# Attention scores: high parts above low parts, and the second product over 64 rows

## The chip, the cores and the metric

The kernel runs on one core of a Trainium2 chip. The metric is the device time of one execution in microseconds; the time before the change is 663.08 us, the median of two runs (663.04 and 663.12). Everything that the text says of single instructions comes from one further execution that the hardware profiler recorded.

## The reference

The reference is a one-layer encoder over 1024 positions (a grid of 16 rows by 64 columns) with 1024 channels: an embedding LayerNorm, one input projection, a neighbourhood attention with 8 heads of 64 channels, a bidirectional gated recurrence, two branch projections with sigmoid gates, an output projection, and a final LayerNorm. All of it is float32. The part that the change touches is the scores of the attention:

```python
q_rows = (q * scale).reshape(B, rows, GRID_W, H, Dh).transpose(1, 0, 2, 3, 4)
...
s = jnp.einsum('bqhd,bqnhd->bhqn', q_row, k_g).astype(jnp.float32) + bias[None]
p = jax.nn.softmax(s, axis=-1).astype(v.dtype)
return jnp.einsum('bhqn,bqnhd->bqhd', p, v_g)
```

Every query of a head has a dot product over 64 channels with the keys of its window (8 rows by 16 columns of the grid); a bias is added, and the softmax over the window weights the values.

## The kernel before, in words

**Tiles.** The 1024 positions are cut into eight tiles of 128 (16 grid rows by 8 grid columns each). The window of a query lies in its own tile and the two beside it (`near`), so a tile's scores are a block of 128 queries by 384 keys, or by 256 keys in the first and the last tile; the bias holds a huge negative number outside the window.

**Two parts of a number.** [...] Most products of the kernel take three (`mm3`, line 129: high by high, low by high, high by low). The scores need two matmuls, because a head has only 64 channels and the array has 128 rows: the 128 rows hold both parts of q.

**Before the attention.** q and k of all heads are projected, split and stored to DRAM (`q_d`, `k_d`: per pair of heads 128 channels, then the part z, then the position).

**Loading a head.** `load_q` (line 925) brings q of one head as 128 rows of 1024 positions. The DRAM view is "(p z) s": row 2p is the high part of channel p, and row 2p+1 its low part. The same function loads the head's bias. `load_k` (line 933) brings k as 128 rows of two times 1024 positions. Rows 2p and 2p+1 hold the same data: the high part of channel p and behind it the low part; the copy is made by a broadcast view of one DMA. q and the bias have one buffer for even heads and one for odd heads; k has two buffers.

**The scores.** `score` (line 1102) issues two matmuls per head and tile into one PSUM bank. Both have the same 128 x 128 block of q as weights. The first has k's high part as the moving operand, so it sums (q high + q low) x k high; the second has k's low part and adds (q high + q low) x k low. That is four products of parts in two matmuls.

**The attention stage.** One loop over units (line 1236 on) writes down the order by hand, on every engine: nothing is reordered by a planner. A unit is one tile of one head: it holds the score of the next head, its bias and row minimum on VectorE (`biased`, line 1109, one DVE instruction out of PSUM), the exponential on ScalarE (`exped`), the transposes of the present head's probabilities on PE (`turned`), their split into two parts (`turned_hi` on ScalarE, `turned_lo` on VectorE), and their product with the values (`values`). Between these, PE does matmuls of the recurrence branch's projection (`filler`, tensor `mb`, line 133), 12 to 20 of them a head. The sums of the softmax are transposed once a head (`sums_turned`, line 1172), with 8 columns of weights.

**Queues.** Nearly all DMAs are issued by SyncE (SP), in program order, each issue waiting in that order for its buffer. At the first unit of head h SP issues the loads of head h+2 (`load_head`): q, bias, k, then the gate `za` of the pair in odd heads; the filler's loads (`wb`, `g`) follow. The scores of head h+2 begin eight units later, at the first unit of head h+1. The loads of heads 0 and 1 are issued in the stage before, at the slots around `HEAD_AT`.

Of the kernel before, what the change touches and what calls it, by code (L numbers as in the profile page):

```python
# [10 lines left out]
F32 = mybir.dt.float32  # L11
# [4 lines left out]
P = 128  # L16
S = 1024
# [3 lines left out]
DH = 64  # L21
# [26 lines left out]
HALVES = ((slice(0, 64), slice(64, P)), (slice(64, P), slice(0, 64)))  # L48
# [3 lines left out]
def near(t):  # L52

    return range(max(t - 1, 0), min(t + 2, NT))
# [13 lines left out]
def encoder_kernel(ctx, tc, x, gb1, gb, w_qk, w_v, w_s, w_ba, w_bb, w_gate, smalls, bias, w_out, out):  # L68
    nc = tc.nc
    V, A, G, PE, SP = nc.vector, nc.scalar, nc.gpsimd, nc.tensor, nc.sync  # L70
# [26 lines left out]
    q_d = dram.tile([H // 2, P, 2, S], F32, name="q_d")  # L97
    k_d = dram.tile([H // 2, P, 2, S], F32, name="k_d")
# [822 lines left out]
    def head_start():  # L921
        late["hd0"] = pool("hd0", "right")
        load_q(0)

    def load_q(h):
        hd = late["hd" if h % 2 else "hd0"]
        q = hd.tile([P, S], F32R, tag="qs", name=f"qs{h}")
        bt = hd.tile([P, BIAS_W], F32, tag="bias", name=f"bias{h}")
        SP.dma_start(q[:].bitcast(F32), q_d[h // 2][HALVES[h % 2][0]].rearrange("p z s -> (p z) s"))
        SP.dma_start(bt[:], bias[h])  # L930
        heads[h] = q, bt

    def load_k(h):
        k = late["hd"].tile([P, 2, S], F32R, tag="ks", bufs=2, name=f"ks{h}")
        SP.dma_start(k[:].rearrange("p z s -> p (z s)").bitcast(F32),
                     k_d[h // 2][HALVES[h % 2][0]].rearrange("p z s -> p (z s)").unsqueeze(1).to_broadcast([DH, 2, 2 * S]))
        heads[h] = heads[h][0], k, heads[h][1]

    def load_head(h):
        if h < H:  # L940
            load_q(h)
            load_k(h)
# [21 lines left out]
    for t, slot in enumerate(LATE_AT[1:]):  # L964
        at(slot, 1, lambda t=t: yb_load(t))
        at(slot + 2, 1, lambda t=t: yb_hi(t))
        at(slot + 3, 0, lambda t=t: yb_lo(t))
    at(HEAD_AT, 1, head_pool)
    at(HEAD_AT, 1, lambda: load_k(0))
    at(HEAD_AT, 1, lambda: load_head(1))  # L970
    at(HEAD_AT - 3, 1, head_start)
# [81 lines left out]
    for slot in range(7 * N_PAIR + 4):  # L1053
        p, k = divmod(slot, 7)
# [47 lines left out]
    def score(h, t):  # L1102
        q, k, _ = heads[h]
        keys = slice(near(t).start * P, near(t).stop * P)
        o = scs[h, t] = pst.tile([P, HALF], F32, tag="s", bufs=2, name=f"s{h}_{t}")
        for z in range(2):
            PE.matmul(o[:, :P * len(near(t))], q[:, t * P:(t + 1) * P], k[:, z, keys], start=z == 0, stop=z == 1)  # L1107

    def biased(h, t):

# [125 lines left out]
    for unit in range(-NT, H * NT + PV_LAG):  # L1236
        h, c = divmod(unit, NT)
# [32 lines left out]
        if -1 <= h < H - 1:  # L1270
            score(h + 1, SCORES[c])
# [44 lines left out]
    def ring(slot, name):  # L1316
        tag = RING[slot % 8]
        return pst.tile([P, HALF], F32, tag=tag, bufs=1 if tag[0] == "a" else 2, name=name)
# [300 lines left out]
    for slot in range(16 + len(plan)):  # L1619
# [17 lines left out]
        if slot < 16:  # L1637
# [3 lines left out]
            o = got[slot] = ring(slot, f"mb{j}{n}")  # L1641
# [6 lines left out]
        a, b, p = plan[slot - 16]  # L1648
# [4 lines left out]
        if slot < 16 + len(plan) - 1:  # L1653
            o = banksX[p] if a in ("a11", "s2", "s3", "a22") else banksW[p]
# [5 lines left out]
    p, x, w = 3, banksX[3], banksW[3]  # L1660
# [11 lines left out]
    for n, part in pieces[2:] + pieces[:2]:  # L1672
        z = zs[p, 1, n]
# [89 lines left out]
```

## Time and profile before

| | |
|---|---|
| median of the runs shown | 663.08 us |
| the profiled execution's own time | 663.5 us |
| its span, first to last instruction | 661.7 us |
| PE busy, share of the span | 649.5 us, 98% |
| weight loads (PEld), which overlap PE | 543.5 us, 82% |
| VectorE (DVE) | 521.6 us, 79% |
| ScalarE (ACT) | 389.0 us, 59% |
| GpSimd (POOL) | 396.7 us, 60% |
| mean granted TensorE clock | 0.996 |
| scores, line 1107: 128 matmuls | 31.7 us busy, mean 329 ns |
| scores' first weight load, last matmul start | 428.2 us, 521.7 us |

How to read it: a line gives the source line, the engine, the operation, the tensors (out<-in), the shapes and the count. For a weight load, `128*128` is rows by columns of the array that it fills. PE's matmuls are pipelined and their ends are modelled, so the step from one start to the next is a better measure of the cost of a matmul than its duration. A wait names the instruction whose end released it.

### The profile page before, as it was taken

How to read it: one execution, taken by the hardware profiler on the slowest of the kernel's cores; microseconds unless marked ns; L12 is line 12 of the kernel's file. 1: busy time of each engine (PE TensorE's matmuls, PEld its weight loads, DVE VectorE, ACT ScalarE, POOL GpSimd, SP SyncE). 2: the span in 40 equal slices, each digit the busy share in tenths (PEclk: the TensorE clock that was granted, in tenths of full speed). 3: DMA queues.
4: the chain of work that ended last, by engine and by line, in shares of the span. 5: the costliest groups of instructions: out<-in, count | busy, mean ns of one | idle time of the engine just before them, and what ended most of it. 6: DMA issues, size and time to landing. Idle time of an engine off the chain costs nothing.

```text
span 661.7 us, 9464 instructions
## 1 busy us (share of the span) xinstructions
PE 649.5 (98%) x3119; PEld 543.5 (82%) x3119; DVE 521.6 (79%) x860; ACT 389.0 (59%) x686; POOL 396.7 (60%) x311
## 2 busy tenths in 40 slices
PE   8999999999999999999999999999999999999994
PEld 7888888888888887888788888888898888888883
DVE  7978867786899599879987696277877876994776
ACT  5564433356786677777666834277777744573242
POOL 6799263434676476658556455013552549989857
PEclk9999999999999999999999999999999999999998
DMA  8747607033334133532361548898977298333023
GB/s 324 271 140 250 195 33 257 15 111 128 125 113 135 57 112 99 188 111 81 132 220 59 192 163 281 306 342 272 362 264 240 68 306 294 113 113 127 24 104 128
DMA packets 52482, 113.42 MB, mean 171 GB/s; under 512 B 5505, under 2 KB 9937, under 8 KB 50897
## 3 DMA queue, kind: packets, MB, share of 16 engines
q1 hardware_dynamic: 51968, 112.28, 49.0%
q8 instruction: 25, 0.41, 0.2%
q10 hardware_dynamic: 464, 0.53, 0.2%
q14 instruction: 25, 0.20, 0.1%
HBM read 77.11 MB, written 35.68 MB: 170 GB/s over the span
## 4 chain that ended last, share of the span: by engine, by line
PE 86%; DVE 7%; POOL 2%; issue 1%; ACT 1%; DMA 1%; POOLq 0%; DVEq 0%; ACTq 0%
PE a L133 32%; PE s L133 12%; PE mb L133 12%; PE x L133 6%; PE w L133 5%; PE v L327 4%; PE s L1107 3%; PE acc L1155 3%; PE pt L1129 3%; PE q L133 2%; PE g L805 2%; POOL x L260 1%; DVE ws_l L127 1%; DVE uc L763 1%; PE tp L271 1%
## 5 line engine op out<-in xcount | busy, mean ns | idle before, releaser
L133 PE MATMUL a<-ht_h,ws_h 128*128 128x512 f32 x136 | 53.1, 391 | 0.0
L133 PE MATMUL a<-ht_l,ws_h 128*128 128x512 f32 x136 | 52.9, 389 | 0.0
L133 PE MATMUL a<-ht_h,ws_l 128*128 128x512 f32 x136 | 52.9, 389 | 0.0
L133 PE MATMUL a<-b_l,wa_h 128*128 128x512 f32 x136 | 52.9, 389 | 0.0
L133 PE MATMUL a<-b_h,wa_h 128*128 128x512 f32 x136 | 52.9, 389 | 0.0
L133 PE MATMUL a<-b_h,wa_l 128*128 128x512 f32 x136 | 52.9, 389 | 0.0
L1117 DVE CUSTOM_DVE_ANT_0 sc<-s,bias 128x384 f32<-128x384 f32 (+1 forms) x64 | 33.5, 523 | 20.3 <-PE s L1107 11.4
L1136 ACT CAST pt_h<-pt 128x384 fp32r<-128x384 f32 x64 | 29.0, 453 | 23.8 <-PE pt L1129 19.3
L1122 ACT ACTIVATE p<-sc,summ 128x384 f32<-128x384 f32 (+1 forms) x64 | 37.9, 592 | 5.4 <-DVE summ L1117 5.0
L133 PE MATMUL mb<-ya,wb_h 128*128 128x512 f32 x128 | 39.7, 390 | 0.1
L913 POOL CAST wb_h<-wb 128x512 fp32r<-128x512 f32 x9 | 7.0, 781 | 47.2 <-DMA wb<-in_w_bb_dram 47.2
L127 DVE TENSOR_TENSOR pt_l<-pt,pt_h 128x384 fp32r<-128x384 f32 x64 | 33.3, 520 | 1.9 <-ACT pt_h L1136 1.6
L127 POOL TENSOR_TENSOR ht_l<-t,ht_h 128x512 fp32r<-128x512 f32 x16 | 21.9, 1406 | 18.2 <-ACT ht_h L313 18.2
L1521 POOL TENSOR_TENSOR z<-z,gb 128x512 f32<-128x512 f32 (+2 forms) x23 | 27.7, 1218 | 8.5 <-ACT z L1516 7.5
L327 PE MATMUL v<-wv,b_h 128*128 128x512 f32 x128 | 32.4, 395 | 0.4 <-ACT b_h L426 0.4
L1107 PE MATMUL s<-ks,qs 128*128 128x384 f32 (+1 forms) x128 | 31.7, 329 | 0.0
L133 PEld LDWEIGHTS a<-ht_h,ws_h 128*128 128x128 f32 x136 | 25.5, 188 | 5.9 <-issue 0.5
L1129 PEld LDWEIGHTS pt<-ident,p 128*128 128x128 f32 x176 | 23.1, 140 | 8.3
L133 PEld LDWEIGHTS a<-ht_l,ws_h 128*128 128x128 f32 x136 | 25.5, 188 | 5.3
L133 PEld LDWEIGHTS a<-b_h,wa_l 128*128 128x128 f32 x136 | 25.5, 188 | 5.3
L133 PEld LDWEIGHTS a<-b_h,wa_h 128*128 128x128 f32 x136 | 25.5, 188 | 5.3
L133 PEld LDWEIGHTS a<-b_l,wa_h 128*128 128x128 f32 x136 | 25.5, 188 | 5.3
(542 smaller groups left out, 2258.9 us busy)
## 6 DMA issues: line engine op xcount, KB each, us to landing
ks<-k_d SPq DMA_DIRECT2D x8, 1024.0 KB, 7.6
h_d<-x SPq DMA_DIRECT2D x8, 512.0 KB, 2.9
v_d<-vs SPq DMA_DIRECT2D x8, 512.0 KB, 3.2
q_d<-q SPq DMA_DIRECT2D x8, 512.0 KB, 3.2
ga_d<-ga SPq DMA_DIRECT2D x16, 256.0 KB, 2.1
gb_d<-gb SPq DMA_DIRECT2D x16, 256.0 KB, 2.4
k_d<-k SPq DMA_DIRECT2D x8, 512.0 KB, 5.1
qs<-q_d SPq DMA_DIRECT2D x8, 512.0 KB, 5.2
```

What stands on the lines that cost most here:

```text
L127: eng.tensor_tensor(lo, full, hi.bitcast(F32), ALU.subtract)
L133: PE.matmul(o, a, b, start=first and i == 0, stop=last and i == len(prods) - 1, skip_group_check=not (first and last))
L327: PE.matmul(vos[i][:], a, wv[kind == "w"][k][:], start=vn[i] == 0, stop=vn[i] == 23)
L805: PE.matmul(o[:, n, :], w[:, 2 * d + b, :], us[b][:, n * HALF:(n + 1) * HALF], start=z == 0, stop=z == 1)
L913: G.tensor_copy(hi[:], st[:])
L1107: PE.matmul(o[:, :P * len(near(t))], q[:, t * P:(t + 1) * P], k[:, z, keys], start=z == 0, stop=z == 1)
L1117: V.tensor_tensor_reduce(s[:, :w], o[:, :w], heads[h][2][:, b0:b0 + w], -1.0, 3.0e38, ALU.add, ALU.min, accum_out=sums[h][0][:, t:t + 1])
L1122: A.activation(probs[h % 2][t][:], scs.pop((h, t))[:, :w], AF.Exp, bias=sums[h][0][:, t:t + 1], scale=-1.0, accum_out=sums[h][1][:, t:t + 1])
L1129: PE.transpose(tp[:, n * P:(n + 1) * P], probs[h % 2][t][:, z * P:(z + 1) * P], ident[:])
L1136: A.copy(pt[0][:, span(b)], tps[h, b][:, :P * len(near(b))])
L1155: PE.matmul(acc[n][:, lo - n * HALF:hi - n * HALF], vvs[h // 2][:, b, h % 2, :], pt[:, a:a + hi - lo], start=b in (1, 6) and z == 0, stop= ...
L1521: G.tensor_tensor(z, z, gbs[c, n][:, part], (ALU.mult, ALU.add)[c])
```

## The change

Three places change. `load_q` fills rows 0 to 63 with the high part of q and rows 64 to 127 with the low part, by two DMAs. `load_k` fills rows 0 to 63 and rows 64 to 127 with the same 64 channels of k (high part, then low part), again by two DMAs in place of one with a broadcast view. `score` takes its first matmul over all 128 rows, as before, which sums (q high + q low) x k high; the second is taken over rows 0 to 63 alone, which adds q high x k low. The product q low x k low is no longer in the sum. Numbers and sizes of the matmuls' columns, all buffers, and the order of the work on each engine stay as they are.

```diff
@@ -926,14 +926,15 @@
         hd = late["hd" if h % 2 else "hd0"]
         q = hd.tile([P, S], F32R, tag="qs", name=f"qs{h}")
         bt = hd.tile([P, BIAS_W], F32, tag="bias", name=f"bias{h}")
-        SP.dma_start(q[:].bitcast(F32), q_d[h // 2][HALVES[h % 2][0]].rearrange("p z s -> (p z) s"))
+        for z, rows in enumerate((slice(0, DH), slice(DH, P))):
+            SP.dma_start(q[rows].bitcast(F32), q_d[h // 2][HALVES[h % 2][0], z])
         SP.dma_start(bt[:], bias[h])
         heads[h] = q, bt
 
     def load_k(h):
         k = late["hd"].tile([P, 2, S], F32R, tag="ks", bufs=2, name=f"ks{h}")
-        SP.dma_start(k[:].rearrange("p z s -> p (z s)").bitcast(F32),
-                     k_d[h // 2][HALVES[h % 2][0]].rearrange("p z s -> p (z s)").unsqueeze(1).to_broadcast([DH, 2, 2 * S]))
+        for rows in (slice(0, DH), slice(DH, P)):
+            SP.dma_start(k[rows].bitcast(F32), k_d[h // 2][HALVES[h % 2][0]])
         heads[h] = heads[h][0], k, heads[h][1]
 
     def load_head(h):
@@ -1103,8 +1104,8 @@
         q, k, _ = heads[h]
         keys = slice(near(t).start * P, near(t).stop * P)
         o = scs[h, t] = pst.tile([P, HALF], F32, tag="s", bufs=2, name=f"s{h}_{t}")
-        for z in range(2):
-            PE.matmul(o[:, :P * len(near(t))], q[:, t * P:(t + 1) * P], k[:, z, keys], start=z == 0, stop=z == 1)
+        for z, rows in enumerate((slice(0, P), slice(0, DH))):
+            PE.matmul(o[:, :P * len(near(t))], q[rows, t * P:(t + 1) * P], k[rows, z, keys], start=z == 0, stop=z == 1)
```

## The prediction

> **What bounds the kernel now.** I read the page first: busy times, then the chain of work that ended last.
>
> ```profile
> span 661.7 us, 9464 instructions
> PE 649.5 (98%) x3119; PEld 543.5 (82%) x3119; DVE 521.6 (79%) x860; ACT 389.0 (59%) x686; POOL 396.7 (60%) x311
> PE 86%; DVE 7%; POOL 2%; issue 1%; ACT 1%; DMA 1%; POOLq 0%; DVEq 0%; ACTq 0%
> PE a L133 32%; PE s L133 12%; PE mb L133 12%; PE x L133 6%; PE w L133 5%; PE v L327 4%; PE s L1107 3%; PE acc L1155 3%; PE pt L1129 3%; PE q L133 2%; PE g L805 2%; POOL x L260 1%; DVE ws_l L127 1%; DVE uc L763 1%; PE tp L271 1%
> ```
>
> PE is busy for 98% of the span and holds 86% of the chain. The scores (L1107) are on the chain themselves, with 3%. A share over the whole span says little about one stage, so the next views are the stretches of the attention stage, 425 to 535 us, and the rows of the score matmuls.
>
> ```profile
> 445.00:455.00 10.00, 10.00 (x64) 9.02 (x63) 7.70 (x23) 7.83 (x23) 1.91 (x2) 1.00 1.00 336
> ...
> sum 110.00, PE 109.85 PEld 96.98 DVE 83.58 ACT 77.82 POOL 42.95; mean PE 9.99 PEld 8.82 DVE 7.60 ACT 7.07 POOL 3.90
> ```
>
> The columns are the stretch and its length, then busy time (and count) of PE, weight loads, DVE, ACT and POOL, then granted clock, DMA share and GB/s. PE works 109.85 of 110 us, at the full clock; the next engine, DVE, works 83.58. So in this stage a microsecond more or less on PE is a microsecond of the kernel, and what DVE, ACT or a transfer gains is worth nothing. The clock is already whole: a cooler array has nothing to win.
>
> ```profile
> L1107 PEld LDWEIGHTS s<-ks,qs x128: 186/188/193, 428.2 to 521.5; 128*128 128x128 f32 x128
> L1107 PE MATMUL s<-ks,qs x128: 277/338/423, 428.4 to 521.7; 128*128 128x384 f32 x96, 128*128 128x256 f32 x32
> L1107 PEldq EVENT_SEMAPHORE  x8: 51/51/51, 424.3 to 508.7; - x8
> ```
>
> There are 128 score matmuls, two for each of 64 scores. The change touches the second of each pair: 48 of 384 columns and 16 of 256.
>
> **Part 1: the second product over 64 rows.** The cost of a matmul in a full stream is the step from start to start.
>
> ```profile
> 472.29 0.40 PE L1107 MATMUL s<-ks,qs 128*128 128x256 f32 x2
> 472.53 0.40 PE L133 MATMUL mb<-yb_h,wb_l 128*128 128x512 f32 x1
> ...
> 475.18 0.52 PE L1107 MATMUL s<-ks,qs 128*128 128x384 f32 x2
> 475.53 0.39 PE L133 MATMUL mb<-yb_h,wb_h 128*128 128x512 f32 x1
> ```
>
> Two matmuls of 384 columns take 475.53 - 475.18 = 0.35 us, 0.175 each; two of 256 take 0.24, 0.12 each. The step follows the columns, and the columns stay. The weight load changes from 128x128 to 64x128. It lies beside the running matmul (the steps of 0.12 and 0.175 contain it), so a shorter one gains nothing. Bounds for a matmul of half the rows: at best it takes half of its step, 48 x 0.0875 + 16 x 0.06 = 5.2 us less in all; at worst it can't be overlapped with its full-row neighbours, which is the first rival below. The trace has no matmul of 64 rows, but two instructions with a part of the array. The nearer one in place, inside this stage, is the transpose of the softmax sums, whose weights fill 8 of 128 columns; the other, at the start of the program, fills 16 of 128 rows.
>
> ```profile
> 449.28 0.49 PE L1129 MATMUL pt<-ident,p 128*128 128x128 f32 x3
> 449.53 0.36 PE L1155 MATMUL acc<-pt_h,vv 128*128 128x256 f32 x1
> ...
> 450.66 0.49 PE L1129 MATMUL pt<-ident,p 128*128 128x128 f32 x3
> 450.99 0.27 PE L1174 MATMUL pt<-ident,sums 128*8 128x128 f32 x1
> 451.02 0.42 PE L1155 MATMUL acc<-pt_h,vv 128*128 128x384 f32 x1
> ```
>
> Without the odd transpose, three transposes and the next matmul's start are 0.25 us apart; with it, 0.36. So it costs 0.11, and that is what each ordinary transpose costs (450.99 - 450.66 is three steps of 0.11). Entering and leaving the 8-column shape adds nothing that can be read.
>
> ```profile
> 450.88 0.09 PEld L1174 LDWEIGHTS pt<-ident,sums 128*8 128x8 f32 x1
> 450.99 0.19 PEld L1155 LDWEIGHTS acc<-pt_h,vv 128*128 128x128 f32 x1
> ```
>
> The full weight load behind it starts at 450.99, together with the odd matmul, which is modelled to run for 0.27: it doesn't wait for that matmul's end.
>
> ```profile
> 2.84 0.31 PE L203 MATMUL clock<-zero 128*128 128x128 bf16 x1
> 3.08 0.18 PEld L414 LDWEIGHTS clock<-ident,gb_row 16*128 16x128 f32 x1 [0.20 <-issue]
> 3.11 0.26 PE L414 MATMUL clock<-ident,gb_row 16*128 16x16 f32 x1
> 3.29 0.10 PEld L203 LDWEIGHTS <-zero 128*128 128x128 bf16 x1
> ```
>
> Here rows are cut. The load of 16 rows starts at 3.08, before the full-row matmul ahead of it ends (2.84 + 0.31 = 3.15), and the next full-row load starts at 3.29, before the 16-row matmul ends (3.11 + 0.26 = 3.37). Neither direction shows a wait for an empty array, though the ends are modelled, the clock was still low there, and this is one instance. I take zero for the 64 second products, by the row inside the stage, and keep -5.2 us as the lower end.
>
> **Part 2: the loads.** For each head SP issues two DMAs more: one of q and one of k. The bytes stay: q 512 KB and k 1024 KB are written to the same rows in halves.
>
> ```profile
> L929 SPq DMA_DIRECT2D qs<-q_d x8: 315/320/587, 405.7 to 496.5; - x8
> L935 SPq DMA_DIRECT2D ks<-k_d x8: 527/535/693, 415.0 to 497.6; - x8
> ```
>
> The added issues take 0.32 + 0.54 = 0.86 us of SP for a head by the medians, if a half costs what the whole does. Behind them SP has the bias, k, the gate `za` and the filler's loads. Whether that costs time depends on how long SP idles afterwards.
>
> ```profile
> 416.68 0.59 SPq L935 DMA_DIRECT2D ks<-k_d  x1
> 419.26 0.32 SPq L706 DMA_DIRECT2D gb_d<-gb  x1
> ...
> 434.42 0.32 SPq L929 DMA_DIRECT2D qs<-q_d  x1
> 435.77 0.69 SPq L935 DMA_DIRECT2D ks<-k_d  x1
> 439.40 0.35 SPq L1179 DMA_DIRECT2D rs_d<-rs  x1
> ...
> 498.79 0.59 SPq L904 DMA_DIRECT2D wb<-in_w_bb_dram  x1
> 501.18 0.32 SPq L1017 DMA_DIRECT2D g<-gb_d  x1
> ```
>
> After k of head 2 SP is free from 436.46 to 439.40, 2.9 us. After the longest train of issues it is free from 499.38 to 501.18, 1.8 us. After the loads of heads 0 and 1 it is free from 417.27 to 419.26, 2.0 us, against three added issues there (k of head 0, q and k of head 1: up to 0.59 + 0.59 + 0.59 = 1.8 us). Each covers what is added; `za`, `wb` and `g` are issued up to 0.9 us later, and PE has no wait of any length for them in the stage now (its idle time is 0.15 of 110 us). The value on PE is zero. Without that cover it would be 0.86 x 8 = 6.9 us.
>
> Next, do q and k still land in time? They are issued a head ahead.
>
> ```profile
> DMA to landing us min/median/max: 4.9/7.6/9.1
> ...
> 446.80 0.19 PEld L1107 LDWEIGHTS s<-ks,qs 128*128 128x128 f32 x1
> ...
> 446.87 0.54 SPq L935 DMA_DIRECT2D ks<-k_d  x1
> ...
> 459.33 0.36 PEld L1107 LDWEIGHTS s<-ks,qs 128*128 128x128 f32 x2
> ```
>
> The first line is k's own landing time, the second the first weight load of head 2's scores; the last two are the issue and the first use of head 3's k. Head 2's k, issued at 435.77, has landed by 444.87 even with the longest landing, 1.9 us ahead of use. The second issues of q and k push the last half back by 0.32 + 0.69 = 1.0 us, so 0.9 us is left. Head 2 has 11.0 us from the issue of k to its use, head 3 has 12.5. So no wait appears, as long as a half with 64 rows moves at the pace of the whole. If not, it is the second rival.
>
> The first product of a head now has to see four transfers landed in place of two. One wait is already an instruction of its own, 51 ns long, once a head. Two more a head would be 16 x 0.051 = 0.8 us; the one before the first score ran at 424.3, 3.9 us ahead of it, and so beside older matmuls. I take zero, and 0.8 us as its upper end.
>
> **The sum.** 0 (columns) + 0 (part of the array) + 0 (SP) + 0 (waits) on the profiled execution's own 663.5 us, which is its span of 661.7 and 1.8 around it. The runs' median, 663.08, is 0.4 below this execution, so the forecast is 663.2 us, with 662 to 665 for this case alone: the 0.8 us of waits and as much again of SP's issues, above, and a microsecond below for what the rows don't resolve.
>
> **The rivals.**
>
> *First: changing between 128 and 64 rows stops the pipeline (slower).* If a weight load of another row count can't be made under the running matmul, it stands in the open, once on the way in and once on the way out: 128 times. By the transposes' step, which is as long as a weight load of 128 columns can be apart from the next, that is 0.11 us each, 14 us in all: 677 us. If the array must also run empty, a score matmul lasts 0.338 and its successor starts after 0.175, so 0.16 more, and the whole load of 0.188 behind it: 0.35 x 128 = 45 us, 708 us. It decides as soon as a switch costs more than 0.10 us. The two partial instructions above speak against it; for it speaks only that none of them has 64 rows amid a stream of 384 columns. [...] I give it 0.12 in full, and 0.05 to a part of it, such as one direction only (665 to 672 us).
>
> *Second: DMAs of 64 rows are slower, and the scores wait for k.* In the loads' stretch the engines move 336 GB/s at a share of 1.00. q and k, 1.57 MB by their shapes, take 4.7 us at that rate; at half of it 4.7 us more. Head 2 would then be late by 4.7 - 0.9 = 3.8 us at worst. With k's median landing of 7.6 us instead of 9.1 the lateness is 2.3 us, and 1.5 us less for a later head, 0.8 us. Over the six heads loaded within the stage that is 5 to 23 us: 668 to 686 us. The trace has a load of 64 rows, the softmax sums, beside loads of 128 rows and the same 256 KB, the gates `g`, in the same stage:
>
> ```profile
> DMA to landing us min/median/max: 3.4/5.9/6.2
> ...
> DMA to landing us min/median/max: 3.5/5.9/9.1
> ```
>
> The first is the 64-row load (rsb), the second the 128-row one (g). They land alike, so I give this 0.06. [...]
>
> *Third: half of the rows takes less time (faster).* Then up to 5.2 us go: 658 us, within 2%. Against it: the steps follow columns alone, and the partial transpose is no cheaper than a whole one. 0.05.
>
> **How the numbers follow.** Zero change 0.72; first rival 0.12 in full and 0.05 in part; second 0.06; third 0.05. The range 661 to 672 us holds the first case, the partial switch and the near ends of the second and third, about 0.8. This kernel's runs tell a change of 2% (13.3 us, beyond 676.3 or below 649.8) from none. Slower than that are the first rival in full and half of the second: 0.15. Nothing reaches 2% faster, 0.01. Within 2%: 0.84.
>
> **What would show it.** Right: the second score matmul listed with 64*128 and 64x384, steps of 0.175 into and out of it, PE still some 109.8 of 110 us busy in the stage, scores from 428 to 522 us. Wrong by the first rival: the 64-row weight load or the full one behind it starts only after the matmul before it, steps above 0.28 us around L1107, and PE or its weight loads idle by "issue". Wrong by the second: waits of PE or its weight loads on `ks<-k_d` at the start of a head, and landings above 11 us. Wrong by the third: a step near 0.09 us.

## The result and the profile after

The changed kernel takes 699.11 us (two runs, 697.86 and 700.36) against 663.08 before: 1.054 times as long, 95% interval 1.046 to 1.062. The forecast of 663.2 us, no change, was wrong by 36 us.

The page of the changed kernel, the lines that answer to those shown of before:

```profile
span 698.6 us, 9488 instructions
PE 682.9 (98%) x3119; PEld 549.2 (79%) x3119; DVE 521.8 (75%) x860; ACT 388.9 (56%) x686; POOL 396.6 (57%) x311
PE a L133 27%; PE mb L133 14%; PE s L133 10%; PE x L133 6%; PE s L1108 5%; PE w L133 5%; PE v L327 4%; PE acc L1156 3%; PE pt L1130 3%; PE q L133 2%; DVE ws_l L127 2%; DMA g<-gb_d 2%; PE g L805 2%; POOL x L260 1%; DVE uc L763 1%
```

PE has as many instructions as before and is still "98% busy": the added time is booked as work. Only the chain betrays a change, with the scores (now L1108) at 5% and a transfer that was not on it, `g<-gb_d`, at 2%.

The score matmuls of before, of after, and of the run with the row change alone (below), from the view of the tile `s`; the two times are the starts of the first and the last of them:

```profile
L1107 PE MATMUL s<-ks,qs x128: 277/338/423, 428.4 to 521.7; 128*128 128x384 f32 x96, 128*128 128x256 f32 x32
```

```profile
L1108 PE MATMUL s<-ks,qs x128: 278/391/687, 432.4 to 558.7; 128*128 128x384 f32 x48, 64*128 64x384 f32 x48, 128*128 128x256 f32 x16, 64*128 64x256 f32 x16
```

```profile
L1107 PE MATMUL s<-ks,qs x128: 277/381/443, 428.5 to 545.4; 128*128 128x384 f32 x48, 64*128 64x384 f32 x48, 128*128 128x256 f32 x16, 64*128 64x256 f32 x16
```

All of the loss lies here. The first score starts 432.4 - 428.4 = 4.0 us later. From first to last score it takes 126.3 us in place of 93.3, 33.0 more. After the last score both kernels have the same 140 us to go (661.7 - 521.7 and 698.6 - 558.7). Together they are the 36.9 by which the span grew, within the rounding of the views. The row change alone takes 116.9 us from first to last score, so of the 33.0 it explains 23.6, and 9.4 are left. These 9.4 lie in the first two heads: from the third head on, both runs take 15.65 us a head.

Two of these three parts are seen in the waits of the changed kernel from 425 to 565 us, and the third in the stretches:

```profile
PEld s L1108 <- issue: 15.7, 64, 0.5
DVE m L1031 <- DMA g<-gb_d: 11.3, 2, 10.7
PEld mb L133 <- issue: 10.6, 51, 0.3
...
PE s L1108 <- DVE m L1031: 4.0, 1, 4.0
```

```profile
435.00:445.00 10.00, 10.00 (x20) 5.42 (x20) 2.70 (x10) 3.43 (x10) 1.20 (x1) 0.50 0.47 169
445.00:455.00 10.00, 10.00 (x27) 6.33 (x26) 3.65 (x12) 2.76 (x9) 0.00 (x0) 0.52 0.59 160
...
465.00:475.00 10.00, 10.00 (x50) 7.05 (x50) 6.62 (x19) 6.21 (x19) 0.17 (x1) 1.00 0.85 209
```

First, each of the 64 scores' 64-row weight loads, and the full-row load behind most of them, starts after idle time that nothing else explains ("issue"). Second, once, PE waits 4.0 us for the instruction `m` of DVE, which frees a bank, and DVE waits for the gate g. Third, in the twenty microseconds after that the granted clock is 0.50 and 0.52 of full speed. "PE 10.00 of 10.00" is printed for all three stretches, with 20, 27 and 50 matmuls in them; the count and the clock tell what the busy time hides.

### The profile page after: what moved, and what is told of

Same layout as the page of the kernel before. It is cut to its first block, busy times and chain, and to the rows that moved or that the text cites. A ratio compares the mean times of both kernels' runs of the same rounds, so it can differ in the third digit from the quotient of the medians.

```text
span 698.6 us, 9488 instructions
## 1 busy us (share of the span) xinstructions
PE 682.9 (98%) x3119; PEld 549.2 (79%) x3119; DVE 521.8 (75%) x860; ACT 388.9 (56%) x686; POOL 396.6 (57%) x311
## 4 chain that ended last, share of the span: by engine, by line
PE 83%; DVE 9%; DMA 2%; POOL 2%; issue 2%; ACT 1%; POOLq 0%; DVEq 0%; ACTq 0%
PE a L133 27%; PE mb L133 14%; PE s L133 10%; PE x L133 6%; PE s L1108 5%; PE w L133 5%; PE v L327 4%; PE acc L1156 3%; PE pt L1130 3%; PE q L133 2%; DVE ws_l L127 2%; DMA g<-gb_d 2%; PE g L805 2%; POOL x L260 1%; DVE uc L763 1%
## 5 line engine op out<-in xcount | busy, mean ns | idle before, releaser
L1108 PE MATMUL s<-ks,qs 128*128 128x384 f32 (+3 forms) x128 | 48.4, 413 | 4.0 <-DVE m L1031 4.0
L1108 PEld LDWEIGHTS s<-ks,qs 128*128 128x128 f32 (+1 forms) x128 | 26.2, 205 | 20.8 <-issue 15.7
L1194 POOL TENSOR_TENSOR za<-za,rsb 128x512 f32<-128x512 f32 x8 | 10.2, 1290 | 41.5 <-DMA rsb<-rs_d 41.5
L1130 PE MATMUL pt<-ident,p 128*128 128x128 f32 x176 | 30.3, 276 | 0.0
```

The costliest lines, as they stand in the source:

```text
L1108: PE.matmul(o[:, :P * len(near(t))], q[rows, t * P:(t + 1) * P], k[rows, z, keys], start=z == 0, stop=z == 1)
L1130: PE.transpose(tp[:, n * P:(n + 1) * P], probs[h % 2][t][:, z * P:(z + 1) * P], ident[:])
L1194: G.tensor_tensor(gates[hp][:, halves[n]], gates[hp][:, halves[n]], rsb[hp][:, halves[n]], ALU.mult)
```

## The experiments

My theory (A) after seeing this: three separate causes. The change between 128 and 64 rows costs PE time at every score; transfers of 64 rows are slow and delay g; and the stall that follows lets the clock fall. The rivals: the row change does it all (B), the loads do it all (C), a 64-row matmul is itself slower (D).

**The row change alone, and the loads alone.** The first run keeps the loads of before and changes the second product; the second run keeps the loads of after and makes both products full.

```diff
-        for z in range(2):
-            PE.matmul(o[:, ...], q[:, t * P:(t + 1) * P], k[:, z, keys], ...)
+        for z, rows in enumerate((slice(0, P), slice(0, DH))):
+            PE.matmul(o[:, ...], q[rows, t * P:(t + 1) * P], k[rows, z, keys], ...)
```

> The loads of before, and the second score product over rows 0 to 63 alone (in this layout these are the high and the low part of channels 0 to 31; channels 32 to 63 are left out of that product). Theory A: after's 36 us are two things, the change between 128 and 64 rows (0.39 us for each of 64 scores by after's steps, 25 us) and, by itself, a stall of PE at 428 us with a low clock behind it, which comes from the loads by halves. Then this run takes 688 us (685 to 691), without the stall and at a clock of 1.00. Rival B: all of it comes from the change of rows, the low clock too: 699 us. Rival C: all of it comes from the loads: 663 us.

> The loads of after (q and k by halves of 64 rows), both score products over all 128 rows; nothing of the computation is left out. Theory A: PE idles about 4 us at 428 us while the gate g of the filler lands behind the halves of k, the clock falls to half and comes back sooner than in after, since full-row matmuls follow without gaps: 668 to 676 us. Rival B: 663 us. Rival C: 699 us.

The row change alone: 686.96 us, ratio 1.036 (1.034 to 1.038), at a clock of 0.995. That is 23.9 us, as theory A had it. The loads alone: 692.33 us (685.6 to 693.9), ratio 1.041 (1.035 to 1.047). The theory had 668 to 676, so the loads cost far more by themselves than I thought. PE's waits in that run, 440 to 560 us, say where:

```profile
PE s L1108 <- DMA ks<-k_d: 15.3, 5, 6.3
PE s L1108 <- issue: 3.0, 1, 3.0
```

The scores of five heads wait for k, up to 6.3 us; a sixth wait, of 3.0 us, stands at the same place of a head without a named cause. The two losses, 24 and 29 us, don't add up to the 36 of the changed kernel, which has no such wait. Its steps are longer, so a head lasts longer (15.65 us against 12.5 to 12.8 from first score to first score), and it starts its scores later; so k lands within it, and the one loss covers a part of the other.

**What of the row change costs.** Two runs with the loads of before: both products over 64 rows, and the second product over 96.

```diff
+        for z, rows in enumerate((slice(0, DH), slice(0, DH))):   # both over 64
+        for z, rows in enumerate((slice(0, P), slice(0, 96))):    # second over 96
```

> The loads of before, both score products over rows 0 to 63 (channels 32 to 63 are left out of the scores). It has twice the 64-row matmuls of the run with the second product alone, and as many changes of rows. Theory A, the change is what costs: as that run, 688 us, with a step of 0.175 us between the two 64-row matmuls. Rival D, a 64-row matmul costs more by itself: twice the loss, 713 us.

> The loads of before, the second score product over rows 0 to 95 (channels 48 to 63 are left out of that product). Theory A, in the form that the array's division costs: 96 rows don't fit into a half of the array, so the array stays whole and the run takes 663 us. Rival D, any matmul of fewer rows than its neighbours costs: 688 us.

Both over 64 rows: 686.21 us, ratio 1.035 (1.033 to 1.037). Twice the 64-row matmuls, the same loss: it goes with the changes, not with the matmuls. Over 96 rows: 663.07 us, ratio 1.000 (0.999 to 1.001), and the scores take as long as before:

```profile
L1107 PE MATMUL s<-ks,qs x128: 277/337/422, 428.3 to 521.8; 128*128 128x384 f32 x48, 96*128 96x384 f32 x48, 128*128 128x256 f32 x16, 96*128 96x256 f32 x16
```

So a matmul of fewer rows than its neighbours is not what costs, and rival D falls. That the array is divided for 64 rows was my theory's assumption: no view shows it, and no run between 64 and 96 rows shows where the cost sets in.

The price in place, PE and then its weight loads in the changed kernel around one score:

```profile
470.35 0.34 PE L1108 MATMUL s<-ks,qs 128*128 128x384 f32 x1
470.62 0.44 PE L1108 MATMUL s<-ks,qs 64*128 64x384 f32 x1
470.99 0.50 PE L133 MATMUL mb<-yb_l,wb_h 128*128 128x512 f32 x1
471.33 0.39 PE L133 MATMUL mb<-yb_h,wb_h 128*128 128x512 f32 x1
```

```profile
470.62 0.18 PEld L1108 LDWEIGHTS s<-ks,qs 64*128 64x128 f32 x1 [0.20 <-issue]
470.99 0.19 PEld L133 LDWEIGHTS mb<-yb_l,wb_h 128*128 128x128 f32 x1 [0.19 <-issue]
471.10 0.19 PEld L133 LDWEIGHTS mb<-yb_h,wb_h 128*128 128x128 f32 x1
```

The steps are 0.27, 0.37 and 0.34 us where before has 0.175, 0.175 and 0.23: 0.40 more for one way in and out, and 0.37 on average (23.6 / 64). Each weight load of the other kind starts together with its own matmul, 0.27 or 0.37 after the matmul ahead of it; in a stream of one kind it starts with the matmul ahead (the load of this score's first matmul at 470.23, as the matmul ahead of that one). So it is no longer made under the running matmul: the two overlap by 0.07 us (470.35 + 0.34 against 470.62), by the modelled end. What it waits for is not shown.

**What of the loads costs.** Three runs. The first has the layout and products of before with as many DMAs as after, each over 128 rows. The second is the loads alone, with the halves for rows 64 to 127 issued from ScalarE's queue. The third is the loads alone with the first two gates g issued ahead of head 1's loads, and no longer behind them.

```diff
+        for c in halves:                       # q in two DMAs of 128 rows
+            SP.dma_start(q[:, c]..., ...[:, c])
+        for z in range(2):                     # k in two DMAs of 128 rows
+            SP.dma_start(k[:, z, :]..., k_d[...][HALVES[...][0], z].unsqueeze(1).to_broadcast([DH, 2, S]))
...
+            (A if z else SP).dma_start(q[rows]..., ...)              # two queues
+            (A if rows.start else SP).dma_start(k[rows]..., ...)
...
+    for n in range(2):                         # early gates
+        at(HEAD_AT, 1, lambda n=n: g_load(1, 0, n))
     at(HEAD_AT, 1, lambda: load_head(1))
```

> The layout and the products of before, but q and k of a head each by two DMAs of all 128 rows (q by halves of its positions, k its high part and its low part), so as many issues and transfers as in after. Theory A: what makes after's loads slow is that a transfer of 64 adjacent rows moves at about 215 GB/s instead of 350 to 400. Then this run takes 663 us (662 to 665), the gate g lands about 9 us after its issue, and no score waits for k. Rival E: it is the number of transfers or issues: 692 us, as with the loads of after alone.

> The loads of after, both products over 128 rows, but the halves for rows 64 to 127 are issued from ScalarE's queue at the same place in the order, so that the two halves are in flight together. If two queues let the halves move side by side: 663 to 668 us. [...]

> The loads of after, both products over 128 rows, and the first two gates g ahead of head 1's loads. Theory A: the first stall (4 us) and its low clock (about 2 us) go, the later waits for k stay: 684 to 688 us. Rival: those waits are a consequence of the first stall, since it shifts the later loads; then 663 to 667 us.

Two full-row DMAs: 664.42 us, ratio 1.0025 (1.0011 to 1.0038), and no score waits for k. The number of transfers is worth 1.4 us, not 29. It shows at the same place: PE has one wait there, 1.7 us for `m`, because g comes later than before.

```profile
PE s L1108 <- DVE m L1031: 1.7, 1, 1.7
```

Two queues: 687.86 us (684.6 to 692.0), ratio 1.038 (1.033 to 1.043), far from the 663 to 668 expected of halves that move side by side and near the 692.33 of the loads alone. But the nearness is in part luck. PE's waits in that run are these:

```profile
PE pt L1130 <- DVE sums L1171: 8.3, 4, 3.9
PE s L1108 <- DVE m L1031: 3.9, 1, 3.9
PE acc L1156 <- DVE attn L1167: 2.7, 4, 0.7
PE s L1108 <- DMA ks<-k_d: 2.4, 3, 1.3
```

The waits of scores for k have shrunk from 15.3 to 2.4 us, and a larger loss has come up at the transposes of the probabilities. ScalarE, which takes up their results, now also has the loads in its order of work and once waits 6.9 us for a transfer there (`pt_h` for `vv<-v_d`); that this is the cause was not tested. So the time of this run doesn't tell how fast the halves move; the rate below does.

With early gates: 690.51 us (689.1 to 699.2), ratio 1.044 (1.038 to 1.051), above the 684 to 688 expected. In its profiled execution, the longest of the four, the first stall is gone, but the first scores of later heads wait instead: 8.9 us are put down to k and 7.0 us to g, which the scores don't read. So these waits are not a consequence of the first stall.

The rates decide it. The stretch from 418 to 422 us, in which the loads of the first heads move and the DMA share is about 1.0; its last column is GB/s. Before, then two full-row DMAs, then after, then two queues:

```profile
418.00:422.00 4.00, 4.00 (x19) 3.33 (x18) 1.16 (x2) 1.38 (x2) 0.00 (x0) 1.00 1.00 401
```

```profile
418.00:422.00 4.00, 4.00 (x19) 3.34 (x18) 0.74 (x2) 1.38 (x2) 0.00 (x0) 1.00 0.97 322
```

```profile
418.00:422.00 4.00, 4.00 (x19) 3.33 (x18) 0.99 (x2) 1.38 (x2) 0.00 (x0) 1.00 0.99 213
```

```profile
418.00:422.00 4.00, 4.00 (x19) 3.32 (x18) 0.93 (x2) 1.38 (x2) 0.00 (x0) 1.00 0.95 205
```

The DMA engines are as busy at 213 GB/s as at 401 (shares of 0.99 and 1.00). Two full-row DMAs move 322 GB/s here and 371 in the next four microseconds. Other transfers are part of each figure, so the pace of one half is an estimate from them: a transfer into 64 adjacent rows moved at about half the pace (213 of 401). Two queues move 205 GB/s here, no more than one. What limits the halves is not shown.

**The stall and the clock.** The changed kernel with the first two gates g ahead of head 1's loads:

> The changed kernel, but the first two gates g of the filler are loaded ahead of head 1's q, bias and k, so that they aren't queued behind them. Theory A: no stall at 428 us, no low clock after it, and only the row changes are left: 687 us (685 to 690). Rival F: the low clock comes from the gaps of the row changes and stays without the stall: 695 us or more.

It took 691.21 us (688.4 to 691.3), ratio 1.042 (1.040 to 1.044), a microsecond above the range, at a clock of 0.995. There is no stall at 428 us and no low clock. What is above the 687 of the row change alone is mainly k: without the delay, three scores wait 3.0 us for it. So the delayed g costs the changed kernel about 8 us on balance (9 between the profiled executions): a stall of 4 us and 9.4 us by the clock, and some 4 us back.

Why did the clock stay low for over 20 us, when PE was "busy" throughout? In the run with the loads alone a stall of the same length was followed by 3.4 us of half clock (a mean of 0.57 from 434 to 438 us, and 1.00 before and after). Two runs put the same stall into kernels with the loads of before, once with the row change and once without, by four copies that nothing reads, queued ahead of g:

```diff
+    scratch = dram.tile([4, P, D], F32, name="scratch")
+    for c in range(4):
+        at(HEAD_AT, 1, lambda c=c: SP.dma_start(scratch[c], h_d[c]))
```

> The loads of before and the second product over rows 0 to 63 (channels 32 to 63 left out of that product), as in the run of the row changes alone; in addition four copies of 512 KB from DRAM to DRAM, which nothing reads, are queued ahead of the first gate g, so that PE stalls before the first score as it does in after. Theory G: after a stall of 4 us or more the clock falls to half, and the gaps of the row changes keep it there for some 24 us, as in after: the stall plus about 9 us over the 687 us without it, 698 to 703 us. Rival H: the low clock of after lasts that long because of its loads; here it comes back within 7 us: 692 to 696 us.

> The kernel before with the same four copies ahead of the first gate g, full rows throughout. Theory G: the same stall, the clock at half for 3 to 7 us and not longer, since the matmuls follow without gaps: the stall plus 2 to 3 us over 663 us, 669 to 674 us. Rival H': a stall here, too, is followed by 20 us or more of the low clock: 675 us or more.

PE waits 4.5 us in both. With the row change: 700.22 us, ratio 1.057 (1.055 to 1.059). With full rows: 669.49 us, ratio 1.009 (1.008 to 1.011). Beyond the stall that leaves about 9 us with the row change (over the 686.96 of the row change alone) and about 2 us without. Stretches of the two, the row change first; the third column from the right is the clock:

```profile
434.00:438.00 4.00, 4.00 (x9) 2.23 (x8) 1.14 (x5) 1.31 (x4) 1.88 (x2) 0.50 0.95 317
438.00:442.00 4.00, 4.00 (x9) 2.19 (x8) 1.13 (x4) 1.41 (x4) 0.00 (x0) 0.50 0.56 219
442.00:446.00 4.00, 4.00 (x9) 2.27 (x9) 1.00 (x4) 1.31 (x4) 0.00 (x0) 0.50 0.00 1
446.00:450.00 4.00, 4.00 (x11) 2.40 (x11) 1.73 (x5) 0.71 (x2) 0.00 (x0) 0.50 0.15 39
450.00:454.00 4.00, 4.00 (x11) 2.54 (x10) 1.24 (x4) 1.95 (x6) 0.00 (x0) 0.50 0.93 301
454.00:458.00 4.00, 4.00 (x19) 2.74 (x18) 1.72 (x7) 2.06 (x6) 0.00 (x0) 0.90 0.41 172
```

```profile
434.00:438.00 4.00, 4.00 (x12) 3.52 (x11) 1.70 (x7) 1.85 (x6) 1.89 (x2) 0.50 0.94 282
438.00:442.00 4.00, 4.00 (x19) 3.46 (x19) 2.48 (x9) 2.39 (x9) 0.00 (x0) 0.88 0.71 264
442.00:446.00 4.00, 4.00 (x27) 3.47 (x26) 3.30 (x13) 3.33 (x11) 0.00 (x0) 1.00 0.68 186
```

By these stretches and those from 430 to 434 us (0.61 and 0.77) the half clock lasts 23.9 us with the row change, as long as in the changed kernel (430.6 to 454.5 us), and 6.8 us with full rows. The loads are those of before in both, so loads by halves aren't needed for the long half clock; the row changes hold it down after the stall. Alone they don't bring it down: without the stall the row changes ran at 0.995. In the changed kernel the full clock came back at 454.5 us, 5.7 us after the transposes of the first head had joined the stream (448.8); whether they are the reason was not tested. PE is printed as busy throughout from 434 to 458 us; no view here shows what the clock goes by.

No run was faster than the kernel before.

## Why the prediction was wrong

**What bounds the kernel: right.** PE was the bound in this stage, and every loss of PE became a loss of the kernel: the 4.0 and 33.0 us above are the 36.9 of the span.

**Part 1, "I take zero for the 64 second products": wrong by 23.6 us**, the largest part. The first rival had the late weight loads, the place and a price of 14 to 45 us, and got 0.12. That the array also runs empty, a part of the 45, no run shows; the runs show 0.37 us for the way in and out. The step that failed is the reading of the 16-row load. I compared its start, 3.08, with the modelled end of the matmul ahead, 3.15, and concluded that it did not wait. The changed kernel shows what waiting looks like: the 64-row load at 470.62 also starts 0.07 ahead of the modelled end (470.35 + 0.34 = 470.69). So a start ahead of the modelled end doesn't show that a load did not wait. The right yardstick is the start of the matmul ahead, with which a load in a plain stream starts; by it the 16-row load came 0.24 late, and the row even carried "[0.20 <-issue]", the same mark as the 64 waits of after. The clock was low there by the lengths of the matmuls, though its record prints 1.00: the one ahead (`clock<-zero`) lasted 0.31 us, the shortest of its kind after 7.7 us 0.22. The input of the 16-row load, issued at 0.7 us, had landed only 2.2 us later, so that wait may have a part in it: the row could not have proven the rival, but it was no evidence against it. The row of the 8-column transpose was read rightly, but it is another shape, `128*8`: a part of the columns and all of the rows. In the changed kernel, too, that transpose costs its step of 0.11 us and no more (three transposes and it from 455.91 to 456.27, 0.36 us, as before). It was nearer in place and farther in kind.

**Part 2, "the value on PE is zero": wrong by 4.0 us of stall**, and by the 9.4 of clock behind it. The issues on SP were nearly right: as many full-row DMAs cost 1.4 us in place of zero, and in the changed kernel the first g is issued at 419.65, as before (419.68). What failed is the premise that halves keep the pace of the whole. The second rival had this and got 0.06, because 64-row and 128-row transfers of 256 KB landed alike, in 5.9 us by the median. Those landings didn't tell the rate; the stretches do, 401 against 213 GB/s. That a half moves at half the rate was no more than the rival's assumption before the runs; they show 0.53 of it, 213 of 401, with other transfers in both figures. The rival also named the wrong victim. It looked at k, and where only the loads are changed the scores do wait 15.3 us for k, within its 5 to 23; but in the changed kernel the one to be late was g, queued behind the loads of two heads. The row for it stood in the trace of before, here with the first score's weight loads, and the row of after behind it:

```profile
427.36 0.69 DVE L1030 SCALAR_TENSOR_TENSOR m<-g,mb 128x512 f32<-128x512 f32 x1 [6.24 <-DMA g<-gb_d]
...
428.15 0.41 PEld L1107 LDWEIGHTS s<-ks,qs 128*128 128x128 f32 x2
```

```profile
431.62 0.69 DVE L1031 SCALAR_TENSOR_TENSOR m<-g,mb 128x512 f32<-128x512 f32 x1 [10.68 <-DMA g<-gb_d]
```

Before, DVE waited 6.2 us for g and was done with `m` at 428.05 (427.36 + 0.69), and the first score's weight load came at 428.15. That cover of 0.1 us was never put beside the added transfer time. In the changed kernel `m` starts 4.3 us later, and the first score 4.0.

**The clock: a step that was missing.** "The clock is already whole" (1.00 in its row) was taken as having nothing to win. It also means something to lose: together with the row changes, a stall of 4 us cost 9.4 us more by the clock than its own length.

**The third rival (faster)** is refuted: twice as many 64-row matmuls took 686.21 us in place of 686.96, and the step between two of them is the 0.17 us of full rows. No run shows a cost of the added waits of PE, the other small term.

The range ended at 672, below both slower rivals' full price. Both came true together, with their first causes as the prediction had worked them out; neither had the clock.

## What to carry to other kernels

Be wary of 64 rows in a dense stream of matmuls of 128: they saved no columns, and here each excursion to 64 rows and back cost 0.37 us, while 96 rows cost nothing (663.07 us, ratio 1.000). Load all 128 rows in one transfer; here two halves of 64 rows moved at about half the pace (213 against 401 GB/s), and what suffers first may be whatever is queued behind them. When a trace lacks the operation in question, judge a nearby row by the yardstick of an undisturbed stream (here the start of the instruction ahead), not by a modelled end, and check that it is alike in kind and size, not only close in place.

## What the runs showed that I had not expected

- The change between 128 and 64 rows cost 0.37 us for each of the 64 scores; 96 rows (ratio 1.000), and the 8 columns of the transpose (0.11 us, its step), show no cost.
- In four runs the clock was at half after a stall of 3.9 to 4.5 us at the first score (with one of 3.0 us, from 465 to 475 us in the run with the loads alone, it stayed at 1.00), and with the row changes it stayed at half: 23.9 us against 6.8 with full rows after the same stall of 4.5 us.
- Losses were not additive: 24 us (rows) and 29 us (loads) gave 36 together, since longer heads and the later start gave k the time to land.
